# Writing the head of a transformer-layer kernel as one fixed order on all engines

## The chip, the core and the metric

The kernel runs on one core of one Trainium2 chip. Its metric is the device time of one execution in microseconds. The core has TensorE (matmuls; its weight loads are listed as PEld), VectorE (DVE), ScalarE (ACT), GpSimd (POOL) and SyncE (SP), whose queue issues nearly all loads of this kernel.

## What is computed

One layer of a diffusion backbone over 512 latent tokens of width 1024, with 256 context tokens, all in float32. The part that the change touches is the head of it:

```
sh1, sc1, g1, sh2, sc2, g2 = modulation(c, w_mod, b_mod)       # silu(c) @ w_mod + b_mod
csh1, csc1, ...            = modulation(c_ctx, w_mod, b_mod)
hx = rms_norm(x, norm1_g) * (1 + sc1) + sh1                    # 512 tokens
hc = rms_norm(ctx, norm1_g) * (1 + csc1) + csh1                # 256 context tokens
q, k, v, u, g = split(hx @ w_in)                               # u: 1024 columns, the conv branch
kc, vc        = split(hc @ w_in[:, k and v columns])
attn = attention over k, kc;   y_b = conformer_conv(u);   x = x + g1 * merge(attn, y_b, g)
x = x + g2 * conv_glu_ffn(rms_norm(x) * (1 + sc2) + sh2);   return rms_norm(x)
```

## The kernel before

Weights lie in device memory as chunks of 128 x 2048 floats (1 MB), in the order of their use. `fetch` (line 185) loads one into a buffer of three that share the tag "raw"; the load is issued on SP. A float32 product is made of three products of halves: `split` (line 180) casts a tile to its high half on ScalarE (line 181), subtracts on VectorE to get the low half (line 182), and `mm3` (line 202) multiplies high by high, high by low and low by high (lines 204 to 206).

The head does this. The four token tiles `xt` (128 tokens each) are loaded (line 476) and normed in place (`normed`, line 300): the sum of squares on ScalarE (302), the mean on VectorE (229) and the power -1/2 on POOL (230), the scaling on VectorE (304). For each of four j, the chunks ("sc1", j) and ("sh1", j) hold 256 columns of the scale and shift weights. `mod_rows` (line 418) multiplies the two conditioning vectors by a chunk. Three chunks (those in `WHOLE`, line 39) are done undivided (line 426); the others on four column tiles of 32 at once (line 431). VectorE copies the row out of PSUM (436), and `to_col2` (line 439) turns it into columns by small matmuls (441). `mod_x` (line 448) makes of these the factors A1 and shifts B1, and A1c and B1c for the context (lines 455 to 460). `rows_x` (line 462) makes two column tiles of hx: eight transposes (403), the Identity activation with A1 and B1 (406), and a split into high and low half. `u_mm` (line 466) multiplies hx by the chunks ("u", 0) and ("u", 1), whose eight tiles k accumulate in four PSUM banks: 24 products for a pair of k, 96 in all.

The order is traced from a string, and a planner then places the instructions of every engine by estimated times, so that ready work of a later step may go ahead of a step that waits:

```
FIRST = "m0 x0 r0 m1 w0 a0 r1 m2 w1 r2 a1 b0 m3 r3 a2 b1 a3 b2 b3"
```

Here m is `mod_x` (shift chunk first, then scale chunk), x the tokens, r `rows_x`, w the load and split of a u chunk, a and b `u_mm` for chunk 0 and 1. After a "w", the next r is queued behind the splits of that chunk (line 484). Behind the head come the gating of u (line 495), the norm of the two context tiles (line 509), the rope tables (lines 513 to 522) and the key/value projection (`project`, line 364), which writes the PSUM banks that u gives back. The projection of queries, attention, the rest of the layer and the channel mixer follow.

Of the kernel before, what the change touches and what calls it, by code (L numbers as in the profile page):

```python
# [9 lines left out]
F32 = mybir.dt.float32  # L10
F32R = mybir.dt.float32r
# [22 lines left out]
CB = 2 * 512 + 32  # L34

FIRST = "m0 x0 r0 m1 w0 a0 r1 m2 w1 r2 a1 b0 m3 r3 a2 b1 a3 b2 b3"
WHOLE = (("sh1", 0), ("sc1", 0), ("sc1", 1))

Q_ORDER = "quqqq|uusfufsfsfsf"
KV_LAG, Q_LAG = 3, 3
# [117 lines left out]
def body(tc, x_d, ctx_d, wts_d, vecs_d, rows_d, rope_d, out_d, at):  # L160
# [4 lines left out]
    def pool(name, bufs=1, stack=es, **kw):  # L165
        return stack.enter_context(tc.tile_pool(name=name, bufs=bufs, reuse_waits="tile", **kw))
# [13 lines left out]
    def split(src, hi, lo):  # L180
        a = S.copy(hi, src)  # L181
        b = V.tensor_tensor(lo, src, hi.bitcast(F32), ALU.subtract)  # L182
        return a.ins, b.ins

    def fetch(name, n=CH):
        raw = wp.tile([P, CH], F32, tag="raw", name="raw", bufs=3)
        nc.sync.dma_start(raw[:, :n], wts_d[at[name], :, :n])
        return raw

# [2 lines left out]
    def weights(name, w, n=CH):  # L192
        raw = fetch(name, n)
        out = []
        for o in range(0, n, 1024):
            m = min(1024, n - o)
            t = hlp.tile([P, 2, 1024], F32R, tag="hl", name="hl", bufs=4)
            done[:] = split(raw[:, o : o + m], t[:, 0, :m], t[:, 1, :m])
            out.append(t[:, :, :m].rearrange("p a (k c) -> p a k c", c=w))
        return out  # L200

    def mm3(out, l, r, start, stop):
        l, r = (a if isinstance(a, tuple) else (a[:, 0], a[:, 1]) for a in (l, r))
# [36 lines left out]
    V.tensor_scalar(bs[:, 8:16], vcol(V_BMOD + 32, 8), 1.0, None, ALU.add)  # L240
    cwh = vcol(V_CW, CT * TAPS)
    V.tensor_scalar(cwh, cwh, 0.5, None, ALU.mult)
    A1, B1, A1c, B1c, A2, B2 = (cst.tile([P, 8], F32, name=f"m{i}") for i in range(6))

    def small(n, tag):
        return cst.tile([P, n], F32, tag=tag, name=tag, bufs=4)
# [14 lines left out]
    def new_part():  # L261
        return cst.tile([P, 512], F32, tag="part", name="part", bufs=2)
# [37 lines left out]
    def normed(xt, xn, junk):  # L300
        ss, rs = small(1, "ss"), small(1, "rs")
        S.activation(junk, xt, AF.Square, accum_out=ss)
        rsqrt(rs, ss, D)
        V.tensor_scalar(xn, xt, rs, None, ALU.mult)
# [63 lines left out]
            mm3(o, src[kk][:, :, tok(t)], w, kk == 0, kk == KT - 1)  # L368

    with ExitStack() as p0:  # L370
        sp = pool("sp", stack=p0)
        kt = lambda: sp.tile([P, 256], F32, tag="kt", name="kt", bufs=8)
        qt = lambda: sp.tile([P, T], F32, tag="qt", name="qt", bufs=4)

# [22 lines left out]
        xt = [cbuf[t][:, 0:D] for t in range(TT)]  # L397
        ct = [y4([P, D]) for t in range(2)]

        def modulated(src, k, a, b, dst, n):  # L400
            pt = trp()
            for t in range(n):
                PE.transpose(pt[:, tok(t)], src[t][:, tok(k)], ident)  # L403
            w = n * P
            h = tmp()
            S.activation(h[:, :w], pt[:, :w], AF.Identity, bias=b[:, k : k + 1], scale=a[:, k : k + 1])
            return split(h[:, :w], dst[:, 0], dst[:, 1])


        cs4 = sp.tile([P, KT, 32], F32, name="cs4")  # L410
        G.memset(cs4, 0.0)
        V.tensor_copy(cs4[:, :, 0:2], cs)
        sel = sp.tile([P, 2], F32, name="sel")
        V.tensor_tensor(sel, ident[:, 0:2], ident[:, 32:34], ALU.add)
        for i in (64, 96):
            V.tensor_tensor(sel, sel, ident[:, i : i + 2], ALU.add)

        def mod_rows(name, j):


            r = fetch((name, j)).rearrange("p (k c) -> p k c", c=256)
            pt = acc()
            if (name, j) in WHOLE:
                n = 2
                for k in range(KT):
                    PE.matmul(pt[0:n, 0:256], lhsT=cs[:, k], rhs=r[:, k], start=k == 0, stop=k == KT - 1)  # L426
            else:
                n = P
                for k in range(KT):
                    q = 32 * (k % 4)  # L430
                    PE.matmul(  # L431
                        pt[q : q + 32, 0:256], lhsT=cs4[:, k], rhs=r[:, k], start=k < 4, stop=k >= 4,
                        tile_position=(0, q),
                    )
            row = sp.tile([n, 256], F32, tag="row", name="row", bufs=2)
            V.tensor_copy(row, pt[0:n, 0:256])
            return row, sel if n == P else ident[0:2, 0:2]

        def to_col2(pt, row):
            for h in range(2):  # L440
                PE.matmul(pt[:, 2 * h : 2 * h + 2], lhsT=row[0][:, tok(h)], rhs=row[1], start=True, stop=True)
            return pt[:, 0:4].rearrange("p (h c) -> p c h", c=2)
# [2 lines left out]
        ub = [[bank(), bank()], [bank(), bank()]]  # L445
        wu = {}

        def mod_x(j):

            s = slice(2 * j, 2 * j + 2)  # L450
            pt = acc()
            r1 = mod_rows("sh1", j)
            r2 = mod_rows("sc1", j)
            sc = to_col2(pt[:, 4:8], r2)
            for i, a in enumerate((A1, A1c)):
                V.tensor_tensor(a[:, s], sc[:, i], bs[:, s], ALU.add)
                V.tensor_tensor(a[:, s], a[:, s], vcol(V_N1, 8)[:, s], ALU.mult)
            sh = to_col2(pt[:, 0:4], r1)
            for i, b in enumerate((B1, B1c)):
                V.tensor_tensor(b[:, s], sh[:, i], vcol(V_BMOD, 8)[:, s], ALU.add)  # L460

        def rows_x(j):
            for k in (2 * j, 2 * j + 1):
                modulated(xt, k, A1, B1, hx[k], TT)

        def u_mm(j, ks):
            for k in ks:
                for i in range(2):
                    mm3(ub[j][i], wu[j][i][:, :, k], hx[k], k == 0, k == KT - 1)

        after = []
        for op in FIRST.split():
            n = int(op[1])
            if op[0] == "x":
                for t in range(TT):
                    nc.sync.dma_start(xt[t], x_d[tok(t), :])
                for t in range(TT):
                    normed(xt[t], xt[t], flat(slot[8 + t]))
            elif op[0] == "m":
                mod_x(n)  # L480
            elif op[0] == "r":
                with ExitStack() as q:
                    for i in after:
                        q.enter_context(tc.issue_after(i))
                    rows_x(n)
            elif op[0] == "w":
                wu[n] = weights(("u", n), P)
                after = list(done)
            else:
                u_mm("ab".index(op[0]), (2 * n, 2 * n + 1))  # L490

        cin = [b[:, 0 : T + TAPS - 1] for b in cbuf]
        cacc = [b[:, CB - T : CB] for b in cbuf]

# [566 lines left out]
```

## Time and profile before

| | us |
|---|---|
| median of 3 runs (838.89 to 839.26) | 839.09 |
| the profiled execution | 838.52 |
| its span, first to last instruction | 836.7 |
| TensorE busy in the span | 818.0 |
| VectorE, ScalarE busy | 566.5, 362.1 |

The page gives busy times over the whole span. The stretches, the timeline, the chain of waits and the groups by source line tell them apart; a group's line is that of the helper that recorded it. An engine that is busy all through a stretch sets its length; the idle time of another one costs nothing there.

### The profile page before, as it was taken

How to read it: one execution, taken by the hardware profiler on the slowest of the kernel's cores; microseconds unless marked ns; L12 is line 12 of the kernel's file. 1: busy time of each engine (PE TensorE's matmuls, PEld its weight loads, DVE VectorE, ACT ScalarE, POOL GpSimd, SP SyncE). 2: the span in 40 equal slices, each digit the busy share in tenths (PEclk: the TensorE clock that was granted, in tenths of full speed). 3: DMA queues.
4: the chain of work that ended last, by engine and by line, in shares of the span. 5: the costliest groups of instructions: out<-in, count | busy, mean ns of one | idle time of the engine just before them, and what ended most of it. 6: DMA issues, size and time to landing. Idle time of an engine off the chain costs nothing.

```text
span 836.7 us, 10190 instructions
## 1 busy us (share of the span) xinstructions
PE 818.0 (98%) x3948; PEld 669.3 (80%) x3948; DVE 566.5 (68%) x979; ACT 362.1 (43%) x700; POOL 25.2 (3%) x50
## 2 busy tenths in 40 slices
PE   6999999999999999999999999999999999999995
PEld 2588888878888888888878988888888888888884
DVE  2578878999999997963855377755244555346565
ACT  3454455789776223523515653333122333213333
POOL 1001010000000000000000000000000000000001
PEclk9999999999999999999999999999999999999999
DMA  8861112020102336573730124542222222222102
GB/s 358 307 268 49 51 56 96 4 99 1 51 1 105 126 149 250 209 280 115 259 144 0 52 101 151 201 151 88 89 101 101 100 101 89 89 100 101 51 1 101
DMA packets 16177, 99.25 MB, mean 119 GB/s; under 512 B 1792, under 2 KB 2048, under 8 KB 6144
## 3 DMA queue, kind: packets, MB, share of 16 engines
q1 hardware_dynamic: 15120, 95.98, 31.1%
q10 hardware_dynamic: 1008, 2.62, 0.9%
q8 instruction: 31, 0.51, 0.2%
q14 instruction: 18, 0.15, 0.1%
HBM read 96.49 MB, written 2.10 MB: 118 GB/s over the span
## 4 chain that ended last, share of the span: by engine, by line
PE 91%; DVE 4%; ACT 2%; DMA 1%; issue 1%; POOL 0%; POOLq 0%; SPq 0%
PE acc L204 24%; PE acc L206 24%; PE acc L205 24%; PE bank L205 3%; PE bank L206 3%; PE bank L204 3%; PE tr L715 2%; DMA raw<-in_wts 1%; PE sc L204 1%; PE sc L206 1%; PE sc L205 1%; PE acc L426 1%; DVE s L182 1%; PE acc L431 1%; PE tr L403 1%
## 5 line engine op out<-in xcount | busy, mean ns | idle before, releaser
L204 PE MATMUL acc<-s,hl 128*128 128x512 f32 (+1 forms) x632 | 242.0, 384 | 0.6 <-ACT s L181 0.6
L206 PE MATMUL acc<-s,hl 128*128 128x512 f32 (+1 forms) x632 | 239.5, 379 | 0.0
L205 PE MATMUL acc<-s,hl 128*128 128x512 f32 (+1 forms) x632 | 239.3, 379 | 0.0
L182 DVE TENSOR_TENSOR hl<-raw,hl 128x1024 fp32r<-128x1024 f32 x118 | 139.1, 1185 | 77.4 <-ACT hl L181 76.9
L181 ACT CAST hl<-raw 128x1024 fp32r<-128x1024 f32 x118 | 119.4, 1021 | 148.9 <-PE acc L206 126.9
L204 PEld LDWEIGHTS acc<-s,hl 128*128 128x128 f32 x632 | 118.7, 188 | 23.6 <-issue 1.0
L205 PEld LDWEIGHTS acc<-s,hl 128*128 128x128 f32 x632 | 119.1, 188 | 22.7 <-issue 1.2
L206 PEld LDWEIGHTS acc<-s,hl 128*128 128x128 f32 x632 | 119.0, 188 | 22.5
L532 DVE SCALAR_TENSOR_TENSOR cb<-cb,vecs 128x512 f32<-128x512 f32 x120 | 88.4, 745 | 1.1
L204 PE MATMUL acc<-hl,s 128*128 128x512 f32 (+1 forms) x212 | 82.3, 388 | 0.2 <-DVE tmp L343 0.2
L206 PE MATMUL acc<-hl,s 128*128 128x512 f32 (+1 forms) x212 | 81.9, 387 | 0.0
L205 PE MATMUL acc<-hl,s 128*128 128x512 f32 (+1 forms) x212 | 81.9, 386 | 0.0
L961 DVE TENSOR_SCALAR tmp<-ap,vecs 128x512 f32<-128x512 f32 x22 | 12.0, 547 | 60.0 <-ACT ap L958 60.0
L958 ACT COPY ap<-acc 128x512 f32<-128x512 f32 x22 | 12.9, 588 | 77.9 <-PE acc L206 77.9
L204 PEld LDWEIGHTS acc<-hl,s 128*128 128x128 f32 x212 | 39.9, 188 | 8.3 <-PE sc L206 0.4
L206 PEld LDWEIGHTS acc<-hl,s 128*128 128x128 f32 x212 | 39.9, 188 | 8.3 <-DVE s L182 0.3
L205 PEld LDWEIGHTS acc<-hl,s 128*128 128x128 f32 x212 | 39.9, 188 | 7.6
L255 DVE SCALAR_TENSOR_TENSOR part<-raw,cs,part 128x512 f32<-128x512 f32 x56 | 41.9, 749 | 1.0
L182 DVE TENSOR_TENSOR s<-tmp,s 128x128 fp32r<-128x128 f32 (+2 forms) x67 | 29.2, 465 | 14.5 <-ACT s L181 14.4
L652 ACT ACTIVATE pr<-sc,ss,qs 128x768 f32<-128x768 f32 x32 | 31.9, 997 | 5.5 <-DVE ss L651 3.6
L964 ACT ACTIVATE tmp<-tmp 128x512 f32<-128x512 f32 x22 | 13.9, 633 | 46.5 <-DVE tmp L963 46.4
L965 DVE TENSOR_TENSOR tmp<-tmp,acc 128x512 f32<-128x512 f32 x22 | 15.1, 686 | 27.9 <-PE acc L206 27.9
(251 smaller groups left out, 1191.0 us busy)
## 6 DMA issues: line engine op xcount, KB each, us to landing
raw<-in_wts SPq DMA_DIRECT2D x78, 1024.0 KB, 4.9
raw<-in_wts SPq DMA_DIRECT2D x8, 768.0 KB, 4.2
cb<-in_x SPq DMA_DIRECT2D x8, 512.0 KB, 7.1
y<-in_ctx SPq DMA_DIRECT2D x2, 512.0 KB, 7.5
raw<-in_wts SPq DMA_DIRECT2D x2, 512.0 KB, 3.9
y<-in_rows ACTq DMA_DIRECT2D x2, 512.0 KB, 4.7
out<-o ACTq DMA_DIRECT2D x4, 256.0 KB, 2.8
out<-o SPq DMA_DIRECT2D x4, 256.0 KB, 2.6
```

Source lines behind the costliest of these rows:

```text
L181: a = S.copy(hi, src)
L182: b = V.tensor_tensor(lo, src, hi.bitcast(F32), ALU.subtract)
L204: PE.matmul(out, lhsT=l[0], rhs=r[0], start=start, stop=False)
L205: PE.matmul(out, lhsT=l[0], rhs=r[1], start=False, stop=False)
L206: PE.matmul(out, lhsT=l[1], rhs=r[0], start=False, stop=stop)
L255: yield V.scalar_tensor_tensor(part, r[:, k], s, part, ALU.mult, ALU.add)
L532: yield V.scalar_tensor_tensor(cacc[i], cin[i][:, j : j + T], w, cacc[i], ALU.mult, ALU.add)
L652: S.activation(pt, sc, AF.Exp, bias=mx, scale=r, accum_out=sm)
L715: PE.transpose(pt[:, tok(t)], pr[h, t][:, tok(s)], ident)
L958: S.copy(ap1[:, 1 : T + 1], a)
L964: S.activation(cv, cv, AF.Gelu_apprx_tanh)
L965: V.tensor_tensor(cv, cv, b, ALU.mult)
```

## The change

The head is written out as one region in which every engine issues its instructions in the order in which they are written; the planner still places what is outside the region. In it:

- the four token tiles are loaded first, then the chunks in the order sc1 0, sh1 0, u 0, sc1 1, sh1 1, u 1, sc1 2, sh1 2, sc1 3, sh1 3; the chunks of scale and shift have five buffers of their own (tag "mraw"), in a pool that is closed at the end of the head, ahead of the pool with the rope tables;
- 32 transposes of the raw token tiles into a PSUM bank that nobody reads stand first on TensorE;
- mean and power -1/2 are done for two token tiles at a time;
- all eight chunks of scale and shift are done on column tiles, the scale chunk ahead of the shift chunk; A1 with A1c, and B1 with B1c, lie in one tile and are written by one instruction each;
- the eight transposes of a pair of column tiles stand between steps of the rows; the splits of the u chunks stand by halves;
- `u_mm` goes by halves of a chunk.

The scratch that is set aside for dynamic DMA is 1024 bytes. The diff, cut to its core:

```
-    def fetch(name, n=CH):
-        raw = wp.tile([P, CH], F32, tag="raw", name="raw", bufs=3)
+    def fetch(name, n=CH, raw=None):
+        if raw is None:
+            raw = wp.tile([P, CH], F32, tag="raw", name="raw", bufs=3)
...
+        def mod_fetch(name, j):
+            return fetch((name, j), raw=hp.tile([P, CH], F32, tag="mraw", name="mraw", bufs=5))
...
+        def scales(j, row):
+            a = A1s[:, :, 2 * j : 2 * j + 2]
+            V.tensor_tensor(a, to_col2(acc(), row), both(bs[:, 0:8], j), ALU.add)
+            V.tensor_tensor(a, a, both(vcol(V_N1, 8), j), ALU.mult)
+
+        def shifts(j, row):
+            V.tensor_tensor(B1s[:, :, 2 * j : 2 * j + 2], to_col2(acc(), row), both(vcol(V_BMOD, 8), j), ALU.add)
...
+        def half_split(raw, t, i):
+            split(raw[:, 1024 * i : 1024 * i + 1024], t[i][:, 0], t[i][:, 1])
+
+        def u_mm(j, ks, i):
+            w = wu[j][i].rearrange("p a (k c) -> p a k c", c=P)
             for k in ks:
+                mm3(ub[j][i], w[:, :, k], hx[k], k == 0, k == KT - 1)
+
+        def rows(j, pts):
+            for k, pt in zip((2 * j, 2 * j + 1), pts):
+                scaled(pt, k, A1, B1, hx[k], TT)
+
+        turns = lambda j: [turned(xt, k, TT) for k in (2 * j, 2 * j + 1)]
+
+        with tc.manual_schedule():
+            for t in range(TT):
+                nc.sync.dma_start(xt[t], x_d[tok(t), :])
+            sc, sh, rw = {}, {}, {}
+            sc[0] = mod_fetch("sc1", 0)
+            sh[0] = mod_fetch("sh1", 0)
+            rw[0] = fetch(("u", 0))
+            sc[1] = mod_fetch("sc1", 1)
+            sh[1] = mod_fetch("sh1", 1)
+            rw[1] = fetch(("u", 1))
+            sc[2] = mod_fetch("sc1", 2)
+            warm = bank()
+            for t in range(TT):
+                for k in range(KT):
+                    PE.transpose(warm[:, tok(k % 4)], xt[t][:, tok(k)], ident)
+            ss, rs = small(4, "ssq"), small(4, "rsq")
+            for t in range(TT):
+                S.activation(flat(slot[8 + t]), xt[t], AF.Square, accum_out=ss[:, t : t + 1])
+            for h in (0, 2):
+                rsqrt(rs[:, h : h + 2], ss[:, h : h + 2], D)
+                for t in (h, h + 1):
+                    V.tensor_scalar(xt[t], xt[t], rs[:, t : t + 1], None, ALU.mult)
+            row = mod_row(sc[0])
+            pts = turns(0)
+            scales(0, row)
+            sh[2] = mod_fetch("sh1", 2)
+            shifts(0, mod_row(sh[0]))
+            sc[3] = mod_fetch("sc1", 3)
+            wu[0], wu[1] = hl_tiles(), hl_tiles()
+            scaled(pts[0], 0, A1, B1, hx[0], TT)
+            half_split(rw[0], wu[0], 0)
+            scaled(pts[1], 1, A1, B1, hx[1], TT)
+            half_split(rw[0], wu[0], 1)
+            u_mm(0, (0, 1), 0)
+            row = mod_row(sc[1])
+            u_mm(0, (0, 1), 1)
+            pts = turns(1)
+            scales(1, row)
+            shifts(1, mod_row(sh[1]))
+            sh[3] = mod_fetch("sh1", 3)
+            rows(1, pts)
+            half_split(rw[1], wu[1], 0)
+            half_split(rw[1], wu[1], 1)
+            u_mm(1, (0, 1), 0)
+            u_mm(1, (0, 1), 1)
+            for j in (2, 3):
+                scales(j, mod_row(sc[j]))
+                u_mm(0, (2 * j - 2, 2 * j - 1), 0)
+                u_mm(0, (2 * j - 2, 2 * j - 1), 1)
+                pts = turns(j)
+                shifts(j, mod_row(sh[j]))
+                rows(j, pts)
+                u_mm(1, (2 * j - 2, 2 * j - 1), 0)
+                u_mm(1, (2 * j - 2, 2 * j - 1), 1)
+            for h in range(2):
                 for i in range(2):
+                    u_mm(h, (6, 7), i)
+
+        ph.close()
+        sp = pool("sp", stack=p0)
...
-    nc = bacc.Bacc("TRN2", target_bir_lowering=False, num_devices=1)
+    nc = bacc.Bacc("TRN2", target_bir_lowering=False, num_devices=1, dynamic_dma_scratch_size=1024)
```

`turned` is the transposes of `modulated`, `scaled` its Identity and split; `mod_row` is the column-tiled branch of `mod_rows` with its copy.

## Rows read from the trace of the kernel before

**Rows 1.** Busy time of each engine, its share of the span, instructions.
```profile
PE 818.0 (98%) x3948; PEld 669.3 (80%) x3948; DVE 566.5 (68%) x979; ACT 362.1 (43%) x700; POOL 25.2 (3%) x50
```
**Rows 2.** Stretches: length, busy us (instructions) by engine, granted clock, DMA share, GB/s.
```profile
25.70:58.00 32.30, 32.30 (x197) 23.65 (x197) 20.48 (x51) 16.54 (x26) 1.59 (x6) 1.00 0.73 276
28.00:836.00 808.00, 798.08 (x3846) 659.46 (x3844) 556.12 (x942) 351.34 (x684) 21.58 (x33) 1.00 0.31 111
```
**Rows 3.** Timeline of TensorE, end of the head: start us, us, engine, line.
```profile
57.79 0.39 PE L206 MATMUL bank<-s,hl 128*128 128x512 f32 x1
58.01 0.39 PE L204 MATMUL bank<-s,s 128*128 128x512 f32 x1
```
**Rows 4.** Loads issued at 1.16 and at 4.33 us: count, size, us to landing.
```profile
raw<-in_wts SPq DMA_DIRECT2D x1, 1024.0 KB, 4.8
...
raw<-in_wts SPq DMA_DIRECT2D x1, 1024.0 KB, 11.8
```
**Rows 5.** By source line, the norm: ns min/median/max, first and last start.
```profile
L302 ACT ACTIVATE s<-cb x4: 1056/1056/1057, 10.0 to 13.7; 128x1024 fp32r<-128x1024 f32 x4
L302 ACT ACTIVATION_READ_ACCUMULATOR s<-cb x4: 186/186/187, 10.9 to 14.7; 128x1 f32 x4
...
L304 DVE TENSOR_SCALAR cb<-cb,rs x4: 745/754/755, 12.9 to 17.8; 128x1024 f32<-128x1024 f32 x4
...
L230 POOL TENSOR_TENSOR rsq<-rsq,mhalf x6: 695/706/1192, 75.3 to 98.0; 128x2 f32<-128x2 f32 x6
```
**Rows 6.** The chain of waits in order of time: start us, us, what.
```profile
6.15 5.50 PE acc L426 x16
...
21.13 3.56 PE acc L426 x16
24.71 0.42 DVE row L436
25.18 0.60 PE acc L441 x4
...
30.96 1.02 PE tr L403 x8
...
32.22 1.00 PE acc L431 x16
...
34.11 0.34 PE acc L441 x4
```
**Rows 7.** By source line, Identity and splits of the head.
```profile
L406 ACT ACTIVATE tmp<-tr,m,m x8: 767/772/781, 19.0 to 46.9; 128x512 f32<-128x512 f32 x8
...
L181 ACT CAST s<-tmp x8: 609/620/625, 20.3 to 48.1; 128x512 fp32r<-128x512 f32 x8
L181 ACT CAST hl<-raw x6: 1040/1046/1052, 21.8 to 54.6; 128x1024 fp32r<-128x1024 f32 x6
...
L182 DVE TENSOR_TENSOR hl<-raw,hl x6: 1201/1219/1226, 25.1 to 57.0; 128x1024 fp32r<-128x1024 f32 x6
```
**Rows 8.** Timeline of SP's queue, loads behind the head.
```profile
33.66 0.90 SPq L510 DMA_DIRECT2D y<-in_ctx  x2
...
35.13 0.52 SPq L516 DMA_DIRECT2D rp<-in_rope  x1
```
**Rows 9.** Timeline of weight loads, first matmuls.
```profile
9.51 0.13 PEld L426 LDWEIGHTS acc<-raw,cs 128*2 128x2 f32 x1 [0.30 <-issue]
9.94 4.63 PEld L426 LDWEIGHTS acc<-raw,cs 128*2 128x2 f32 x22 [0.30 <-issue]
```
**Rows 10.** Timeline of the last matmul, and the stretch after 832.6 us.
```profile
827.72 0.28 PE L206 MATMUL acc<-hl,s 128*128 128x256 f32 x1
...
832.60:836.00 3.40, 0.00 (x0) 0.00 (x0) 0.36 (x1) 0.33 (x1) 0.00 (x0) 0.50 0.41 157
```
**Rows 11.** Timeline of ScalarE, the split of chunk u 1.
```profile
34.45 2.00 ACT L181 CAST hl<-raw 128x1024 fp32r<-128x1024 f32 x2 [4.14 <-DMA raw<-in_wts]
...
36.35 1.44 ACT L406 ACTIVATE tmp<-tr,m,m 128x512 f32<-128x512 f32 x2
```

More of the change, by code (lines that the diff above doesn't have):

```diff
@@ L34 @@
 CB = 2 * 512 + 32
-FIRST = "m0 x0 r0 m1 w0 a0 r1 m2 w1 r2 a1 b0 m3 r3 a2 b1 a3 b2 b3"
-WHOLE = (("sh1", 0), ("sc1", 0), ("sc1", 1))
 Q_ORDER = "quqqq|uusfufsfsfsf"
@@ L242, in body @@
     V.tensor_scalar(cwh, cwh, 0.5, None, ALU.mult)
-    A1, B1, A1c, B1c, A2, B2 = (cst.tile([P, 8], F32, name=f"m{i}") for i in range(6))
+    A1s, B1s = (cst.tile([P, 2, 8], F32, name=f"m{i}") for i in range(2))
+    A1, A1c, B1, B1c = A1s[:, 0], A1s[:, 1], B1s[:, 0], B1s[:, 1]
+    A2, B2 = (cst.tile([P, 8], F32, name=f"m{i}") for i in range(2, 4))
     def small(n, tag):
@@ L370, in body @@
     with ExitStack() as p0:
-        sp = pool("sp", stack=p0)
+        ph = ExitStack()
+        hp = pool("hp", stack=ph)
         kt = lambda: sp.tile([P, 256], F32, tag="kt", name="kt", bufs=8)
@@ L398, in body, with turned @@
         ct = [y4([P, D]) for t in range(2)]
-        def modulated(src, k, a, b, dst, n):
+        def turned(src, k, n):
             pt = trp()
@@ L403, in modulated, with scaled @@
                 PE.transpose(pt[:, tok(t)], src[t][:, tok(k)], ident)
+            return pt
+        def scaled(pt, k, a, b, dst, n):
             w = n * P
@@ L407, in modulated @@
             return split(h[:, :w], dst[:, 0], dst[:, 1])
-        cs4 = sp.tile([P, KT, 32], F32, name="cs4")
+        def modulated(src, k, a, b, dst, n):
+            return scaled(turned(src, k, n), k, a, b, dst, n)
+        cs4 = hp.tile([P, KT, 32], F32, name="cs4")
         G.memset(cs4, 0.0)
         V.tensor_copy(cs4[:, :, 0:2], cs)
-        sel = sp.tile([P, 2], F32, name="sel")
+        sel = hp.tile([P, 2], F32, name="sel")
         V.tensor_tensor(sel, ident[:, 0:2], ident[:, 32:34], ALU.add)
@@ L416, in body, with mod_row @@
             V.tensor_tensor(sel, sel, ident[:, i : i + 2], ALU.add)
-        def mod_rows(name, j):
-            r = fetch((name, j)).rearrange("p (k c) -> p k c", c=256)
+        def mod_fetch(name, j):
+            return fetch((name, j), raw=hp.tile([P, CH], F32, tag="mraw", name="mraw", bufs=5))
+        def mod_row(raw):
+            r = raw.rearrange("p (k c) -> p k c", c=256)
             pt = acc()
[L423 to L437, printed above, removed]
+            for k in range(KT):
+                q = 32 * (k % 4)
+                PE.matmul(
+                    pt[q : q + 32, 0:256], lhsT=cs4[:, k], rhs=r[:, k], start=k < 4, stop=k >= 4,
+                    tile_position=(0, q),
+                )
+            row = new_part()[:, 0:256]
+            V.tensor_copy(row, pt[:, 0:256])
+            return row, sel
         def to_col2(pt, row):
@@ L446, in body @@
         wu = {}
[L448 to L466, printed above, removed]
-            for k in ks:
-                for i in range(2):
[L469 to L490, printed above, removed]
+        both = lambda v, j: v[:, None, 2 * j : 2 * j + 2].broadcast_to([P, 2, 2])
@@ new lines, in scales, with hl_tiles @@
+        def scales(j, row):
[4 more added lines that the diff above has]
+            V.tensor_tensor(B1s[:, :, 2 * j : 2 * j + 2], to_col2(acc(), row), both(vcol(V_BMOD, 8), j), ALU.add)
+        def hl_tiles():
+            return [hlp.tile([P, 2, 1024], F32R, tag="hl", name="hl", bufs=4) for _ in range(2)]
+        def half_split(raw, t, i):
+            split(raw[:, 1024 * i : 1024 * i + 1024], t[i][:, 0], t[i][:, 1])
@@ new lines, in u_mm @@
+        def u_mm(j, ks, i):
+            w = wu[j][i].rearrange("p a (k c) -> p a k c", c=P)
+            for k in ks:
+                mm3(ub[j][i], w[:, :, k], hx[k], k == 0, k == KT - 1)
[16 more added lines that the diff above has]
+            for t in range(TT):
+                for k in range(KT):
+                    PE.transpose(warm[:, tok(k % 4)], xt[t][:, tok(k)], ident)
[39 more added lines that the diff above has]
+            for h in range(2):
+                for i in range(2):
+                    u_mm(h, (6, 7), i)
```

## Prediction

> **What bounds the kernel now.** I read the page's busy line first: TensorE 818.0 of 836.7 us [rows 1]. A share of 98% says that TensorE is the bound on the whole, but not where; so the second view is the busy time by stretch. From 25.7 to 58.0 us TensorE is busy 32.30 of 32.30 us, and from 28 us to the end 798.1 of 808, nearly all of the rest being the tail after the last matmul [rows 2]. What is left idle lies before 25.7 us. The third view is the timeline of TensorE at the end of the head: the last product of the u projection (line 206, bank<-s,hl) starts at 57.79 us and the first of the key/value projection (bank<-s,s) at 58.01 us [rows 3]. All behind that mark is the same work in both kernels, with TensorE as its bound, so a shift of the mark is a shift of the end. The question is one number: when does the key/value projection start after the change? Before it is 58.0 us.
>
> **The change part by part.** I follow the new order station by station, each engine strictly in the order written, with durations of the trace of before.
>
> *Landings.* Today the first 1 MB chunk lands 4.8 us after its issue at 1.16, at 6.0; the token tiles land 1.25 us apart (their squares start from 10.0 to 13.7), and the 1 MB chunk behind the last of them at 4.33 + 11.8 = 16.1, so 1 MB takes 2.46 us [rows 4, 5]. With tokens first the four tiles land at 4.75, 6.0, 7.25 and 8.5, then sc0 at 11.0, sh0 13.4, u0 15.9, sc1 18.3, sh1 20.8, u1 23.3, sc2 25.7. Five buffers of their own for the chunks of scale and shift let these go out without a wait; sh2, sc3 and sh3 follow by 33.
>
> *Tokens.* The square of the last tile ends at 8.5 + 1.06 + 0.19 less overlap = 9.7. The mean and the POOL power on two columns take 0.15 and 0.70 to 1.19 (I take 0.9), two scalings 0.69 + 0.75 [rows 5]: 12.3 us. The 32 added transposes of raw tokens (0.11 us each at full clock) lie in a stretch where TensorE has nothing else before 11.0: cost nothing, and 0.6 us if they run at half rate.
>
> *First scale and shift.* Eight transposes 0.9, or 1.02 with the switch behind them (13.2), row to columns 0.34, row of sh0 1.00, copy by VectorE 0.42, to columns 0.60 with its end [rows 6], one tiny addition 0.15 and some hops: 16.0 us. All eight rows are now column-tiled at 1.0 us; the three undivided ones cost 3.56 us each, the first 5.50 [rows 6]. That saves over 9 us of TensorE, all of it ahead of 25.7.
>
> *First products.* ScalarE now does Identity 0.77, cast 0.51, u0's first half 1.0, Identity, cast, u0's second half [rows 7]: the first product can start at 18.4 (25.7 before), but the low halves from VectorE (1.2 us each) and the second column tile stall it; the first six products end at 21.1. Then row sc1 (22.1), six products (23.5), transposes (24.4), to columns, row sh1, copy, to columns, addition: 27.1 us.
>
> *The hole.* The next TensorE instruction is a product with u1's weights. Their cast is written behind Identity and cast of column tiles 2 and 3, which wait for this addition, although u1 landed at 23.3: 2 x 1.3 + 1.05 = 3.7 us on ScalarE [rows 7]. TensorE has been idle since 26.8 and starts at 30.8; behind it wait all rows and products to come. The low halves arrive at 32.1 and 33.2, and the twelve products end at 34.4.
>
> *The rest.* From 34.4 on there are left 72 products x 0.23 = 16.5 [rows 3], 4 rows 4.0, 16 transposes 1.8, 4 times to columns 1.4 [rows 6], and new waits: each of these four rows is directly followed by its own to-columns step, which waits for the copy, 0.17 + 0.42 + hops = 0.67. The planner of before covers such waits with products (TensorE busy throughout, rows 2); in the fixed order no product may move up into them. 4 x 0.67 = 2.7, and 0.8 for first products after a switch and for the last column tile. Sum 27.2: the mark comes at **61.6 us, 3.6 later**. Before, at 34.4 the rest was 58.0 - 34.4 = 23.6: it had done 17 products against 24, but six rows against four and three pairs of transposes against two, and had no waits left.
>
> *Two credits and a cover.* Work from outside the fixed part may fill a wait. The context's transposes do fit: four take half of eight's 0.9 us [rows 6], the context lands by 36 (two 512 KB tiles behind sh3), and one pair fits a 0.67 wait: 0.4 us, from none to all sixteen (1.8 with switches). Fewer tiny VectorE instructions per row are worth 0.1 each, and are in the sum. The rope table (line 516) may have to wait for the memory of the last mod row, 52.0 at the latest; kv's chunk is queued behind it on SP [rows 8], so it lands by 52.5 + 0.5 + 4.8 = 57.8 and is split by 59.2: covered by 2.4 us of the later mark, and gone with it if the mark came before 59. The smaller scratch and the joint tiles have no instruction: nothing.
>
> *Sum:* +3.6 - 0.4 = +3.2. The profiled execution would go from 838.52 (span 836.7 and 1.8 around it) to 841.7; it lies 0.57 under the median of the runs, so I add 3.2 to 839.09: **842.3 us**.
>
> **The clock, weighed.** The weight loads of line 426 come 0.43 us apart until 9.94 and 0.21 apart after it (22 in 4.63) [rows 9]: TensorE ran at 1.2 GHz for 3.8 us of its first matmuls and then at 2.4 GHz. No row shows whether transposes alone lift it. The Trainium skill, TensorE: Matmul & The Clock Gate, Part 4 (PE-mode transpose), says they do not: the full clock does not engage in transpose mode. The trace cannot confirm or deny it. It would speak against this change, whose first TensorE work is 32 transposes, and it is the first rival.
>
> **The rivals.** *(a) The clock stays at 1.2 GHz beyond 11 us.* Rows, transposes and products then take twice their time. If it rises at about 13 us, the same chain gives a mark of 63.1; if only after 20 us, 66.2. With the 0.4 credited: 843.8 to 846.9, 845.5 in the middle. For it: nothing but transposes runs before 11 us. Against it: before it rose while TensorE was simply busy.
>
> *(b) The clock falls in the hole.* At the end of the kernel TensorE's last matmul starts at 827.72, and from 832.6 the granted clock is 0.50 [rows 10]: an idle time of 4.6 us ended so. The hole is 4.0 us, so it may or may not. By [rows 9] the half rate lasts 3.8 us of work, 1.9 us lost: 844.2.
>
> *(c) The other side: the hole does not arise,* because u1's casts do not stand behind Identity on ScalarE, that is, the written order does not hold there. It decides whether they run before 26.8 us (u1 lands at 23.3). The chain then gives a mark of 57.7, the waits of the rest eating nearly all of the earlier start; with the fill 838.4, from 837 with all of the fill to 839. For it: before, ScalarE ran both casts of u1 at 34.45 and Identity behind them at 36.35 [rows 11].
>
> *(d) The fill is large:* the context comes early and all its transposes go into waits, 1.8 us instead of 0.4: 840.9. Against it: its loads stand behind 14 others on SP, and before they were issued at 33.66 behind all ten weight chunks of the head [rows 8].
>
> **How the numbers follow.** Chances: forecast 0.45, (a) 0.22, (b) 0.08, (c) 0.14, (d) 0.06, and 0.05 for outside work with a late input that blocks VectorE or ScalarE within the fixed part (843 to 846). The forecast alone: 841.2 to 843.7, from the power of 0.70 or 1.19 us and the fill. The range reaches from the middle of (c), 838.2, to the end of (a), 846.9. Within 0.2% (about what a measurement can tell from no change) is 837.4 to 840.8. Faster: part of (c) with a full fill, 0.10. Same: the rest of (c), half of (d) and the forecast's lower tail, 0.13. Slower: 0.77.
>
> **What would show it.** In the profile after: token tiles land from 4.8 to 8.5; first product near 18.4; TensorE idle about 4 us near 27 to 31, ended by ScalarE's cast of u1; four waits near 0.67 us for the row copy; the first key/value product at 61 to 62. If weight loads before 20 us come at half rate, (a) holds; if products after 31 us are 0.43 apart, (b); if the cast of u1 ends before 27 us, (c). The forecast is wrong if the mark comes before 59.5, or if later stages absorb its shift, of which I see no sign in a TensorE that is busy 798 of 808 us.

## The result, and the profile after

The kernel after takes 848.97 us (median, 848.12 to 849.23), the kernel before on the same chip 839.15 (838.89 to 839.26): a ratio of 1.0108, 95% interval 1.0095 to 1.012. The forecast was 842.3 us with a range up to 846.9: the sign was right, the size was a third of the true one, and the time lies outside the range. The profiled execution of after is the one of 848.12 us, with a span of 846.3 us; against 836.7 before that is 9.6 us more. The kernel before isn't always at 839: beside the last two experiments three of its 14 executions take 842.6 to 843.3 us, at a mean granted clock of 0.992 instead of 0.994 to 0.998.

The first view is the page of after: the busy line, and the granted clock in 40 slices.

```profile
PE 817.3 (97%) x3980; PEld 672.6 (79%) x3980; DVE 566.8 (67%) x965; ACT 362.9 (43%) x700; POOL 24.7 (3%) x48
...
PEclk9799999999999999999999999999999999999999
```

TensorE is busy for about as long as before, 817.3 us against 818.0 [rows 1], in a span that is 9.6 us longer. It is not the same work: over 9 us of undivided rows are gone, 32 transposes are new, and what runs at a lower clock is busy for longer. So the added time shows as idle time, with slow time hidden in the busy time, and the clock is lowest in the second slice, 21 to 42 us, in the head. The measure of the prediction was the start of the key/value projection; here is the timeline of TensorE around it in after.

```profile
66.16 0.39 PE L204 MATMUL bank<-s,hl 128*128 128x512 f32 x1
66.39 0.39 PE L202 MATMUL bank<-s,s 128*128 128x512 f32 x1
```

The mark stands at 66.39 us, against 58.01 before [rows 3]: 8.4 of the 9.6 us are lost ahead of it, 1.2 behind it (846.3 - 66.39 = 779.9 against 836.7 - 58.01 = 778.7). The third view cuts the head of after at the places where the granted clock changes (columns: stretch; its length, then busy us and instructions of PE, PEld, DVE, ACT and POOL; granted clock, DMA share, GB/s).

```profile
4.90:9.59 4.69, 4.67 (x21) 4.22 (x22) 1.14 (x6) 3.33 (x6) 0.76 (x1) 1.00 1.01 385
9.59:19.83 10.24, 5.70 (x62) 4.21 (x61) 4.72 (x12) 3.78 (x7) 1.14 (x5) 1.00 1.01 427
19.83:23.25 3.42, 3.23 (x10) 1.39 (x13) 2.92 (x3) 1.98 (x3) 0.00 (x0) 0.50 1.02 426
23.25:30.07 6.82, 5.29 (x54) 3.65 (x46) 1.34 (x5) 0.75 (x1) 0.00 (x0) 1.00 1.01 419
30.07:36.90 6.83, 3.79 (x8) 2.58 (x9) 3.75 (x4) 4.30 (x7) 0.00 (x0) 0.50 0.95 386
36.90:66.40 29.50, 26.49 (x175) 19.40 (x175) 13.02 (x32) 12.73 (x21) 1.54 (x6) 1.00 0.36 148
```

Twice, from 19.83 to 23.25 and from 30.07 to 36.90, TensorE runs at the lower of its two levels, 1.2 GHz. Before, the clock was at 1.00 from 9.96 us on to the end of the matmuls. (Ahead of its first record, the rise at 9.59, the view shows 1.00, though the transposes there come at half rate: 21 in 4.69 us.) What TensorE waited for in after (total us, times, longest):

```profile
PE bank L202 <- ACT hl L178: 6.7, 2, 4.0
...
PE acc L446 <- DVE part L441: 4.1, 6, 1.4
...
PE tr L360 <- DVE tmp L344: 1.0, 1, 1.0
```

The first line is two waits for a cast of u weights: 2.66 us ahead of the first product at 19.62, and the hole of 3.99 us that ends at 33.07. TensorE's timeline in after at that hole:

```profile
28.48 0.61 PE L446 MATMUL acc<-sel,part 128*128 128x2 f32 x4 [0.55 <-DVE part L441]
33.07 0.80 PE L202 MATMUL bank<-s,hl 128*128 128x512 f32 x1 [3.99 <-ACT hl L178]
```

The timeline of ScalarE in after shows what it is made of.

```profile
29.32 0.78 ACT L411 ACTIVATE tmp<-tr,m,m 128x512 f32<-128x512 f32 x1 [7.47 <-DVE m L461]
...
31.98 1.99 ACT L178 CAST hl<-raw 128x1024 fp32r<-128x1024 f32 x2
```

ScalarE had been idle for 7.47 us ahead of 29.32, waiting for the addition of shift 1 (L461), while chunk u1 lay in its buffer from 24.55. Its cast comes last, at 31.98, because it is written last.

### The profile page after: what moved, and what is told of

Its sections match the earlier page's. It is cut to its first block, busy times and chain, and to the rows that moved or that the text cites. A ratio compares the mean times of both kernels' runs of the same rounds, so it can differ in the third digit from the quotient of the medians.

```text
span 846.3 us, 10241 instructions
## 1 busy us (share of the span) xinstructions
PE 817.3 (97%) x3980; PEld 672.6 (79%) x3980; DVE 566.8 (67%) x965; ACT 362.9 (43%) x700; POOL 24.7 (3%) x48
## 4 chain that ended last, share of the span: by engine, by line
PE 89%; DVE 4%; ACT 3%; DMA 2%; issue 1%; POOL 0%; SPq 0%; POOLq 0%; ACTq 0%
PE acc L202 24%; PE acc L204 24%; PE acc L203 24%; PE bank L204 3%; PE bank L202 3%; PE bank L203 3%; PE tr L765 2%; PE sc L202 1%; PE sc L204 1%; PE sc L203 1%; DMA mraw<-in_wts 1%; PE acc L436 1%; DVE s L179 1%; DMA raw<-in_wts 1%; DVE hl L179 1%
```

## The experiments

Each kernel is compared with the kernel before on its own chip. The first four are from one chip (before: 839.26, 838.55 to 841.65), the next three from a second (840.28, 838.98 to 840.91), the last two from a third (839.81, 838.97 to 843.26). All were made after reading the profile of after, so their theories begin with the hole and with the two falls of the clock. e2, e3 and e5 were run twice, e6 three times, the others four to ten times. Marks and half-rate times in the text are those of the profiled executions.

| kernel | median, us | ratio to before, 95% | mark, us | at 1.2 GHz behind the first rise, us |
|---|---|---|---|---|
| after | 848.97 | 1.0108 (1.0095 to 1.012) | 66.39 | 10.2 |
| e1_split_early | 843.53 | 1.0044 (1.003 to 1.0057) | 61.36 | 6.8 |
| e2_fill_holes | 851.49 | 1.0133 (1.0103 to 1.0162) | 69.92 | 6.8 |
| e3_no_warm | 850.57 | 1.0122 (1.0081 to 1.0162) | 68.66 | 13.7 |
| e4_planner | 844.18 | 1.0055 (1.0038 to 1.0072) | 63.34 | 10.2 |
| e5_before_cols | 845.04 | 1.0062 (1.0041 to 1.0083) | 64.90 | 20.5 |
| e6_early_fill | 843.15 | 1.0031 (1.0014 to 1.0049) | 62.87 | 3.4 |
| e7_pipelined | 836.40 | 0.9958 (0.9942 to 0.9975) | 55.90 | 0 |
| e9_no_fill | 837.88 | 0.9969 (0.9955 to 0.9983) | 56.09 | 3.4 |
| e10_pipelined_again | 835.59 | 0.9948 (0.9932 to 0.9965) | 54.45 | 0 |

### Take the hole away: e1_split_early

The two splits of u1 move ahead of the factors and shifts of column tiles 2 and 3. Nothing else changes.

```
             pts = turns(1)
+            half_split(rw[1], wu[1], 0)
+            half_split(rw[1], wu[1], 1)
             scales(1, row)
             shifts(1, mod_row(sh[1]))
             sh[3] = mod_fetch("sh1", 3)
             rows(1, pts)
-            half_split(rw[1], wu[1], 0)
-            half_split(rw[1], wu[1], 1)
```

> Only edit: the two half splits of chunk u 1 stand ahead of the to-columns step of scale chunk 1, so ScalarE casts u1 when it lands (24.6 us) and not behind Identity of column tiles 2 and 3. Theory H+C (the hole of 4.0 us is the written order on ScalarE, and the second fall of the clock, 30.1 to 36.9 us, comes from the hole): TensorE goes on at about 29 us at 2.4 GHz, 4.0 + 1.9 = 5.9 us faster than the changed kernel, about 843. Rival H alone (the clock falls there anyway, from the light work ahead of it): 4.0 faster, about 845. Rival N (another input, not u1's cast, ends the hole): no change, 849.

Measured: 843.53 us (842.13 to 844.59), 5.4 less than after, of which 5.0 are ahead of the mark. The hole is gone; TensorE's timeline goes from the to-columns of shift 1 straight to a product with u1.

```profile
29.59 0.61 PE L446 MATMUL acc<-sel,part 128*128 128x2 f32 x4 [0.55 <-DVE part L441]
30.05 0.48 PE L202 MATMUL bank<-s,hl 128*128 128x512 f32 x1
```

The gain is more than the 4.0 us of the hole, as the theory that also counts the slow products behind it asks: after 30.05 they come 0.23 us apart. The clock did fall once, earlier than in after (stretches ahead of the first fall, and at half rate):

```profile
11.86:18.68 6.82, 4.54 (x52) 3.05 (x50) 2.75 (x7) 1.30 (x2) 0.53 (x5) 1.00 1.02 430
18.68:25.51 6.83, 5.70 (x24) 2.67 (x25) 4.26 (x5) 4.07 (x6) 0.00 (x0) 0.50 1.01 423
```

So more than half of the loss is this one written order of two lines, together with the slow products behind it. 4.3 us of loss remain without the hole.

### Keep the holes, but fill them: e2_fill_holes

Both waits stay where they are. 20 transposes go into the first and 15 products of the weights of u0 into the second, into spare banks; their results are not used.

```
             half_split(rw[0], wu[0], 1)
+            spare = acc()
+            for n in range(20):
+                PE.transpose(spare[:, tok(n % 4)], xt[n % 4][:, tok(n % 8)], ident)
             u_mm(0, (0, 1), 0)
...
             half_split(rw[1], wu[1], 1)
+            spare = acc()
+            w = wu[0][0].rearrange("p a (k c) -> p a k c", c=P)
+            for n in range(15):
+                PE.matmul(spare, lhsT=w[:, 0, n % 8], rhs=hx[0][:, 0], start=True, stop=True)
             u_mm(1, (0, 1), 0)
```

> Only edit: 20 transposes into a spare bank in the first hole (17.0 to 19.6 us) and 15 products into a spare bank in the second (29.1 to 33.1 us), work that nobody reads; both holes stay as long as they are. Theory C (idle time and light work let the clock fall twice, and that costs beside the holes): granted clock 1.0 from about 10 us on, some 0.8 us back at the first and 1.9 at the second, about 846.3. Rival (the half clock lies under the holes and costs nothing, or it falls whatever TensorE does): 849, with the clock at 0.5 as before.

Measured: 851.49 us (851.48 to 851.51), 2.5 more than after, which neither of the two theories forecast. The part on the clock came out, the total did not. The stretches of e2: from the first row to the second hole's end, the twelve products behind that hole, and a later one.

```profile
13.80:33.40 19.60, 17.09 (x139) 11.89 (x131) 8.01 (x17) 8.27 (x12) 0.44 (x4) 1.00 1.01 422
33.43:37.26 3.83, 3.30 (x16) 2.17 (x20) 2.34 (x2) 0.90 (x1) 0.00 (x0) 1.00 1.04 409
51.35:58.18 6.83, 5.97 (x16) 4.88 (x17) 3.55 (x8) 0.84 (x2) 0.00 (x0) 0.50 0.12 29
```

With work in both holes the clock holds through them, and the twelve products behind the second take 3.83 us; in after they take 5.02 (33.07 to 38.09). That is 1.2 us for the second fall, measured. But a new wait stands at 49.2 to 52.2 us: the to-columns of sc3 wait 2.99 us for the copy of the row (L441), and VectorE's timeline in e2 shows why.

```profile
48.24 0.75 DVE L305 TENSOR_SCALAR y<-y,rs 128x1024 f32<-128x1024 f32 x1 [0.67 <-POOL rs L228]
...
50.47 0.75 DVE L305 TENSOR_SCALAR y<-y,rs 128x1024 f32<-128x1024 f32 x1 [0.67 <-POOL rs L228]
...
51.74 0.42 DVE L441 COPY part<-acc 128x256 f32<-128x256 f32 x1
```

The norm of the context (L227, L305) is not in the fixed part. The planner put it on VectorE ahead of the copy, where it twice waits 0.67 us for POOL. In that wait the clock fell a first time in e2, at 51.35, and the twelve products behind it took 5.4 us, against 3.0 in after. Up to this wait the fill did pay: from the first product to the row of sc3 e2 takes 27.5 us (20.65 to 48.15), after 29.4 (19.62 to 48.98). Then the wait takes 1.6 us more than in after and the products 2.4 more, and e2 had begun its products 1.0 later, since in that execution TensorE waited 0.96 us between two token tiles and its clock rose only at 13.80. So e2 shows what a fall costs; by its total, filling is no gain.

### No transposes of raw tokens: e3_no_warm

The 32 transposes that the change puts first are left out; their results are used nowhere.

```
-            warm = bank()
-            for t in range(TT):
-                for k in range(KT):
-                    PE.transpose(warm[:, tok(k % 4)], xt[t][:, tok(k)], ident)
```

> Only edit: the 32 transposes of raw tokens that open TensorE's work are left out. Theory W (transposes alone did lift the clock at 9.6 us): without them the clock rises only after the rows of chunk 0, about 16 us or later, and the time is 0.5 to 2.6 us longer, 849.5 to 851.5. Rival (the clock rose on its own, or transposes do not count for it): it rises at the same time and the kernel stays at 849.

Measured: 850.57 us (849.51 to 851.62). The interval overlaps that of after, so the time doesn't tell the two apart; the mark is 2.3 us later in the profiled executions. The clock does (stretches of e3 from its first matmul on):

```profile
12.60:15.56 2.96, 2.96 (x21) 1.76 (x22) 1.45 (x3) 0.00 (x0) 0.33 (x3) 1.00 1.02 429
...
18.98:25.80 6.82, 4.53 (x22) 2.15 (x22) 3.83 (x4) 4.41 (x6) 0.00 (x0) 0.50 1.01 424
```

Without the transposes TensorE starts at 12.60 and the rise is recorded at 15.56; in after it stands at 9.59, behind nothing but transposes. They do lift the clock. They don't keep it: in both kernels it falls soon after, at 18.98 and at 19.83.

### The same steps, placed by the planner: e4_planner

The steps and their order as written stay; the region that holds every engine to that order does not.

```
-        with tc.manual_schedule():
+        if True:
```

> Only edit: the same steps, tiles, buffers and loads, traced in the same order, but without the fixed region: the planner may move ready work up. Theory O (the fixed order is the loss, not the tokens first, the column tiles or the buffers): the holes and the copy waits are covered, the clock holds, and the time is near the kernel before, 838 to 842. Rival L (the loss comes from what the steps are, above all the later landing of chunks behind tokens): 845 to 849.

Measured: 844.18 us (842.74 to 845.72): 4.8 less than after, and still 5 more than before. The planner covers most of the waits (the copies cost TensorE 1.1 us in all instead of 4.1, the casts of u 0.8 instead of 6.7; 2.1 us for ScalarE's Identity are new), but not the clock, which falls twice (stretches of e4):

```profile
20.48:27.31 6.83, 6.00 (x22) 2.26 (x22) 3.48 (x4) 2.20 (x3) 0.00 (x0) 0.50 1.01 420
...
34.14:37.55 3.41, 3.41 (x9) 2.43 (x9) 3.24 (x4) 2.14 (x3) 0.00 (x0) 0.50 1.04 409
```

Half of the loss goes with the fixed order, and half stays. That does not make the steps as such the cause of the other half: e7, below, has the same steps and loads in another fixed order and is faster than before. The next run takes out the one step that I had credited most.

### The kernel before with column tiles only: e5_before_cols

One line of the kernel before: no row is multiplied undivided any more. It is the one part of the change by which I had credited over 9 us of TensorE.

```
-WHOLE = (("sh1", 0), ("sc1", 0), ("sc1", 1))
+WHOLE = ()
```

> The kernel before with one edit: no chunk of scale or shift is done undivided, all eight on column tiles (one part of the change alone). Theory D (the three undivided rows, 3.6 to 5.5 us of dense matmuls each, are what keeps the clock at 2.4 GHz up to the first products in the kernel before): the granted clock is 0.5 in some stretch between 10 and 32 us, which gives back the 7.5 us of TensorE saved; 838 to 843. Rival (the undivided rows are only slow): the clock holds, the first product starts some 2 us sooner, and the time is 836 to 838.

Measured: 845.04 us (844.02 to 846.06), 1.0062 of before: TensorE has less to do and the kernel is some 5 us slower. First a stretch of the kernel before, then two of e5:

```profile
9.96:13.55 3.59, 3.59 (x18) 1.45 (x17) 1.14 (x3) 3.41 (x6) 0.55 (x1) 1.00 1.04 428
```

```profile
10.14:13.55 3.41, 0.88 (x11) 0.26 (x3) 1.24 (x3) 3.09 (x5) 0.56 (x2) 1.00 1.04 428
13.55:27.20 13.65, 9.09 (x51) 5.37 (x54) 4.68 (x15) 5.87 (x10) 1.99 (x7) 0.50 0.61 247
```

Up to 13.55 us the undivided row of before keeps TensorE busy all the time (3.59 of 3.59 us). In e5 it is busy 0.88 of 3.41 us, the rest is waiting, and the clock falls at 13.55 and comes back at 27.20; from 30.62 to 37.44 it is down once more. The dense rows saved nothing by going: they lay in a time when weights were still landing, and the clock held with them.

Not all of the 4.8 us need be the clock, since with this edit the planner places the other engines anew. The first product starts at 29.63 us instead of 25.71, and one reason is the norm, whose last token tile is scaled by 20.71 instead of 18.54. POOL's timeline in e5 shows part of that: a power of the norm (L230) stands behind a memset for the conv (L502) that waits for TensorE's transposes.

```profile
17.32 0.11 POOL L502 MEMSET cb<- 128x15 f32 x1 [1.76 <-PE tr L403]
17.39 0.55 POOL L230 TENSOR_TENSOR rs<-rs,mhalf 128x1 f32<-128x1 f32 x1
```

The power behind it stands so too, at 19.38. How the loss divides between the clock and this order no run shows.

### The second hole removed, the first filled: e6_early_fill

e1, with 20 transposes in the wait ahead of the first product. Their results are not used.

```
             half_split(rw[0], wu[0], 1)
+            fill(20)
             u_mm(0, (0, 1), 0)
...
+            half_split(rw[1], wu[1], 0)
+            half_split(rw[1], wu[1], 1)
             scales(1, row)
...
```

> The kernel with u1 split early, and beside it 20 transposes that nobody reads, in the hole ahead of the first product. The hole itself stays. Theory C (light work ahead of the first product lets the clock fall at about 19 us, and the half rate costs what its products and rows take longer, about 2 us of the 3.3 + 1.9 + 1.9 us that they took): clock 1.0 from about 12 us on, 841 to 842 where that kernel took 843.5. Rival (the half rate lies under waits for VectorE's low halves): 843.5.

Measured: 843.15 us (841.17 to 843.49), by its interval not to be told from e1, and nearer to the rival's 843.5 than to the 841 to 842 of the theory. The clock holds through the first hole, and the first six products take 2.79 us (19.01 to 21.80) against 3.33 in e1. But TensorE then waits 3.0 us for a row copy, from 26.6 to 29.6, and the timelines of VectorE and TensorE in e6 show two low halves of u1, now written early, ahead of that copy:

```profile
26.58 2.36 DVE L179 TENSOR_TENSOR hl<-raw,hl 128x1024 fp32r<-128x1024 f32 x2 [3.29 <-ACT hl L178]
...
29.12 0.42 DVE L441 COPY part<-acc 128x256 f32<-128x256 f32 x1
...
29.60 0.73 PE L446 MATMUL acc<-sel,part 128*128 128x2 f32 x4 [3.00 <-DVE part L441]
```

The clock fell at 29.93, behind that wait. In e1 the same low halves were done by 28.2 us, before the copy was due at 29.1: its u1 was cast from 24.73 on, here from 25.50, as it landed, while the row was ready earlier here. The total is inconclusive; e6 shows that e1's move is not free: with u1's casts early, their low halves can stand in front of what TensorE needs next.

### A fixed order without the waits: e7_pipelined, e9_no_fill, e10_pipelined_again

If the loss is the order and the light work, a fixed order that has neither should be no slower than the planner's. e7 writes each row, then six products or eight transposes of work that is ready, then the to-columns that need the copy of that row; it splits u1 behind row sh1, and the work with no use (27 transposes into a bank of u that is cleared later) goes where nothing is ready.

```
...
-            shifts(0, mod_row(sh[0]))
+            row = mod_row(sh[0])
+            fill(5)
+            shifts(0, row)
...
-            u_mm(0, (0, 1), 0)
+            fill(22)
             row = mod_row(sc[1])
-            u_mm(0, (0, 1), 1)
+            u_mm(0, (0, 1), 0)
             pts = turns(1)
             scales(1, row)
-            shifts(1, mod_row(sh[1]))
+            row = mod_row(sh[1])
             sh[3] = mod_fetch("sh1", 3)
-            rows(1, pts)
             half_split(rw[1], wu[1], 0)
             half_split(rw[1], wu[1], 1)
+            u_mm(0, (0, 1), 1)
+            shifts(1, row)
             u_mm(1, (0, 1), 0)
+            row = mod_row(sc[2])
+            rows(1, pts)
             u_mm(1, (0, 1), 1)
...
```

The rest of the order follows the same pattern.

> A fixed order again, same steps and loads as the changed kernel, but written so that no step of TensorE stands directly behind what it waits for: row of scale 1 ahead of the first products, u1 split early, each copy of a row covered by six products or eight transposes, each rows step by more than 3.6 us of other work, and transposes that nobody reads in the two first waits. Theory O (a fixed order as such costs nothing; the loss is where the waits were put, and the clock): products from about 20 us, TensorE busy behind them, key/value projection from about 55 us, 836 to 838, faster than the kernel before. Rival P (every fixed order loses to the planner, which reacts to landing times): 840 to 844.

Measured: 836.4 us (836.14 to 836.96), 0.9958 of before (0.9942 to 0.9975): 3.5 to 4 us faster than before, and 12.6 less than after. The head from 20 us to the mark, in e7:

```profile
20.00:55.90 35.90, 35.03 (x241) 25.78 (x242) 20.58 (x44) 19.93 (x30) 1.55 (x6) 1.00 0.76 307
```

TensorE is busy 35.03 of 35.90 us at full clock. The six waits for a row copy, 4.1 us in after, are one of 0.2. To see what the fill is worth by itself, e9 leaves the 27 transposes out of e7, and e10 is e7 again, on the same chip as e9.

```
-            fill(5)
...
-            fill(22)
```

> The pipelined order with one edit: the 27 transposes that nobody reads (5 under the copy of shift row 0, 22 ahead of scale row 1) are left out, so TensorE idles some 0.5 and 2.6 us there; nothing else moves. Theory C (the clock is a price of its own): it falls at the first products, near 20 us, and the products of the next 3.4 to 6.8 us take twice as long: 1.5 to 3.5 us slower than the pipelined kernel beside it. Rival (with every wait covered, the fill was not needed): within 0.5 us of it.

> The pipelined order once more, unchanged, on the same chip as the kernel without its fill, for their difference: 836 to 837, 2.5 to 3 us under the kernel before.

Measured: e9 837.88 us (836.69 to 838.93), e10 835.59 us (834.97 to 836.54): the fill brings 2.3 us, and the two sets of times don't touch. e10 is 4.2 us under the kernel before, more than the 2.5 to 3 expected. A stretch, the row of sc1 and two products of e9, then the same of e10:

```profile
20.91:24.32 3.41, 3.41 (x15) 2.14 (x8) 2.69 (x4) 1.47 (x2) 0.00 (x0) 0.50 1.03 425
```

```profile
20.23 1.33 PE L436 MATMUL acc<-mraw,cs 128*32 128x256 f32 x16 [2.75 <-DMA mraw<-in_wts]
...
22.51 0.63 PE L204 MATMUL bank<-s,hl 128*128 128x512 f32 x1
22.94 0.63 PE L202 MATMUL bank<-s,hl 128*128 128x512 f32 x1
```

```profile
19.66:54.45 34.79, 34.56 (x240) 25.78 (x241) 20.50 (x44) 19.91 (x30) 1.54 (x6) 1.00 0.80 319
```

```profile
19.66 1.07 PE L436 MATMUL acc<-mraw,cs 128*32 128x256 f32 x16 [0.30 <-DMA mraw<-in_wts]
...
21.23 0.40 PE L204 MATMUL bank<-s,hl 128*128 128x512 f32 x1
21.47 0.39 PE L202 MATMUL bank<-s,hl 128*128 128x512 f32 x1
```

Without the fill TensorE waits 2.75 us ahead of the row of sc1, the clock falls at 20.91, and the six products then start 0.42 to 0.60 us apart; with it they start 0.23 to 0.33 apart. From the start of that row to the transposes behind the six products e9 takes 3.99 us (20.23 to 24.22) and e10 2.53 (19.66 to 22.19): 1.5 us for the half rate, of which 0.4 is caught up later. The row itself starts 0.6 later in e9, since sc1 landed later in that execution. Together the mark is 1.6 us earlier with the fill (54.45 against 56.09). The other 1.4 us between the two profiled executions (spans of 833.1 and 836.1) lie behind the mark; 1.0 of it is the wait of L360 that after has too. So by these two traces the clock's share is 1.1 to 1.5 us, and about as much lies behind the mark, where the clock is the same in both.

## Why the prediction was right in sign and wrong in size

Right:
- *The measure.* The start of the key/value projection carries 8.4 of the 9.6 us.
- *The hole.* Forecast 26.8 to 30.8 with 4.0 us, ended by ScalarE's cast of u1; measured 29.08 to 33.07 with 3.99, ended by that cast. Rival (c), that the written order would not hold there, is out.
- *The row copies.* Forecast four waits of 0.67; three of those four took 0.55, the fourth comes below. The chunks land 2.46 to 2.50 us apart (forecast 2.46), the row of a column-tiled chunk takes 1.04 to 1.10 us at full clock (forecast 1.0).

Wrong, in the order of the chain; the errors on the mark add up to 4.8 us (forecast 61.6, measured 66.39):

*Landings, +1.2.* I let the tokens land at 4.75, 6.0, 7.25 and 8.5 us, from the 1.25 us between two tiles in the trace of before. That spacing was of tiles in the middle of a busy queue. ScalarE's squares in after start as the tiles land:

```profile
4.80 1.06 ACT L499 ACTIVATE s<-cb 128x1024 fp32r<-128x1024 f32 x1 [1.58 <-DMA cb<-in_x]
...
6.74 1.06 ACT L499 ACTIVATE s<-cb 128x1024 fp32r<-128x1024 f32 x1 [0.79 <-DMA cb<-in_x]
...
8.47 1.06 ACT L499 ACTIVATE s<-cb 128x1024 fp32r<-128x1024 f32 x1 [0.58 <-DMA cb<-in_x]
...
9.70 1.06 ACT L499 ACTIVATE s<-cb 128x1024 fp32r<-128x1024 f32 x1
```

The first tile was right, the next came 1.94, 1.73 and 1.23 us apart; sc0 landed at 12.12 instead of 11.0, and the first product started at 19.62 instead of 18.4. The term also varies from one execution to another: with the same loads the first row, which waits for sc0, starts at 11.63 in e6 and at 12.79 in e9.

*The clock, +2.0.* I had it as rival (b) with a chance of 0.08, with one fall, in the hole of 4.0 us, since the only fall in the trace of before stood 4.6 us behind the last matmul [rows 10]. It fell twice. The second time was in that hole, but at 30.07, only 1.0 us after the last matmul; the twelve products behind it took 5.02 instead of the forecast 3.6 us, +1.4 (e2, with the clock held: 3.83, so 1.2 of it is the clock, where (b) had priced a fall at 1.9). The first time I had not thought of: at 19.83, behind a wait of 2.66 us in a chain of rows, transposes and to-columns. The first six products took 3.3 instead of 2.7 us, +0.6 (e6, with the clock held, against e1: 0.5). The step that failed is "an idle time of 4.6 us ended so. The hole is 4.0 us, so it may or may not": I weighed the length of one idle time against one row, and left out what TensorE had done ahead of it. In the heads of after and of e1 to e10 the clock falls twelve times. Nine times it falls in a wait of 2.5 to 4.0 us or within 0.7 us behind one; three times (both in e4, the second in e5) among rows, small matmuls and transposes with no wait over 1.1 us. None needed 4.6 us.

Behind this stands a step that I had as a gain: "That saves over 9 us of TensorE, all of it ahead of 25.7." It saved them, and they were worth less than nothing: e5 makes this saving alone and loses 5 us, by the clock and by the order that the planner then chose. In before a busy TensorE in a time when data was still landing cost nothing, and the clock held.

*Rival (a)*, that the clock would stay at 1.2 GHz beyond 11 us because only transposes run, is out for after: the 32 transposes began at 4.92 and the rise stands at 9.59; without them it stands at 15.56 (e3). The Trainium skill, TensorE: Matmul & The Clock Gate, Part 4 (PE-mode transpose), says that the full clock does not engage in transpose mode; the measurement says otherwise for these float32 transposes. That the rise came so early was in part luck with the landings. Of the eight profiled executions with these transposes, the three in which TensorE never waited between token tiles have the rise at 9.02 to 9.59 (after, e6, e10), the five with a wait of 0.64 to 1.37 us there at 10.67 to 13.80 (e9, e1, e7, e4, e2; in e4 and e2 with the first row already begun).

*The rest, +1.1* (38.09 to 66.39, 28.3 us instead of 27.2). 0.7 of it is the wait of sc3's to-columns, 1.37 us instead of 0.67. VectorE's timeline in after has the same block as in e2, here with the row complete at 50.05 (its last matmuls end there):

```profile
47.08 0.75 DVE L305 TENSOR_SCALAR y<-y,rs 128x1024 f32<-128x1024 f32 x1 [0.66 <-POOL rs L228]
...
49.07 0.75 DVE L305 TENSOR_SCALAR y<-y,rs 128x1024 f32<-128x1024 f32 x1 [0.67 <-POOL rs L228]
49.74 1.28 DVE L179 TENSOR_TENSOR s<-tmp,s 128x512 fp32r<-128x512 f32 x2
50.94 0.42 DVE L441 COPY part<-acc 128x256 f32<-128x256 f32 x1
```

Outside work with a late input that blocks VectorE within the fixed part was in the prediction with 0.05, together with all else of its kind. The other three waits were 0.12 cheaper each; what is left, 0.8, is spread over rows, to-columns and one context transpose with its two switches (0.25, at 61.54).

*The credit of 0.4* did not come: of the context's transposes one ran ahead of the mark, and not in a wait.

*Behind the mark, +1.2.* I took this part as the same work. It has one wait that before did not have, the query's transposes (L360) on VectorE (L344), 1.0 us at 131 us. e1, e2, e4 and e9 have it, e3, e6, e7 and e10 do not, though behind the mark all of them do the same work; e9 and e10 differ by 27 transposes alone. The order in which the planner places the work does not explain it: behind the mark TensorE, VectorE, ScalarE and POOL run the same instructions in the same order in e9 and in e10. One line of TensorE's timeline in e9, then the same transposes in e10:

```profile
121.17 0.63 PE L360 MATMUL tr<-ident,qt 128*128 128x128 f32 x4 [1.03 <-DVE tmp L344]
...
118.38 0.60 PE L360 MATMUL tr<-ident,qt 128*128 128x128 f32 x4
```

In e9 the transposes wait for an instruction of VectorE (L344, at 120.34) that comes 2.5 us behind the last one to finish a query tile before them (L346, at 117.88); in e10 they do not. Why the same order comes with a different wait stays open.

The three parts together: forecast +3.6 on the mark, 4.8 of errors on it (1.2 landings, 2.0 clock, 1.1 rest, 0.5 small sums in the chain between), 1.2 behind it: 9.6 us.

The range failed by construction. It took each rival by itself; (b) and the blocked VectorE came together, on top of late landings that were in no rival, and none of them excluded another.

## What to carry to other kernels

Time saved on an engine in a stretch where it waits anyway is no gain, and on TensorE it can be a loss, as in e5: look at the granted clock around such a stretch, and if it falls there, keep the dense form or put work into the wait (in e10, 27 unused transposes took away a slow stretch that cost 1.1 to 1.5 us in e9). In an order fixed by hand, write next on each engine what will be ready next, and put independent work between a producer and the step that waits for it: the same steps in after's order took 848.97 us, and in e9's 837.88. And look at what a planner may still push into an in-order engine between fixed steps, since a step with a late input there holds up all behind it.

## What the hardware showed that I had not expected

- Transposes alone lifted TensorE's clock (they began at 4.92, the rise is recorded at 9.59; later where TensorE waited between them, up to 13.80 in e2), and 27 of them, 22 in a wait of 2.75 us, kept it (e10 against e9).
- The clock fell in after at 30.07, 1.0 us behind the last matmul, where TensorE had done rows on column tiles, small matmuls and transposes with short waits; at the end of the kernel before, behind dense products, it fell 4.6 us behind the last [rows 10].
- The first loads of this kernel were slower than the same loads behind others: token tiles landed 1.94 and 1.73 us apart at the start of after (ScalarE's squares start 1.49 and 1.48 apart in e6, 2.87 in e7), 1.25 apart behind other loads [rows 5]. The transfer rates in after, in 40 slices of 1 us from 0 on, stay below 420 GB/s until 9 us.

```profile
GB/s 0 41 290 336 299 360 340 410 397 442 418 434 418 434 434 426 418 434 434 418 434 410 426 434 410 426 401 426 410 442 410 434 406 385 430 390 234 337 432 426
```

In the same view the kernel before, with a 1 MB chunk first, moves 377 to 426 GB/s from 3 to 12 us. Whether the size of the tiles or their number at once makes the difference was not tried.
